# Seven-product units: two passes with the same weights as one product of 512 columns

## The chip, the core and the metric

The kernel runs on one core of one Trainium2 chip. The metric is the device time of one execution in microseconds; before the change it is 1432.15 us, the median of three runs from 1432.05 to 1433.4. Five engines work side by side: PE (TensorE, matmuls), DVE (VectorE), ACT (ScalarE), POOL (GpSimd) and SP, which here issues loads. Each goes through its own list of instructions in order and waits on semaphores for the others.

## What is computed

Two decoder layers over 512 tokens of 1024 channels, in float32. Layer 0 begins with a recurrent and pooling mixer, layer 1 with a convolution module; each layer then has cross-attention into 256 memory tokens and a gated MLP, which is the part that the change is about. Cut to it:

```
D_MODEL, SEQ, D_FF = 1024, 512, 3 * 1024

def rms_norm(x, g):
    y = x * rsqrt(mean(x * x, -1) + EPS)
    return y * g

def conv_ffn(x, norm, w_up, dw_w, dw_b, w_down):
    h = rms_norm(x, norm) @ w_up                       # 1024 -> 6144
    g = causal_dwconv(h[..., :D_FF], dw_w, dw_b)       # width 3
    u = h[..., D_FF:]
    return (gelu(g) * u) @ w_down

x = x + conv_ffn(x, ...)
```

## The kernel before

Activations are held transposed: 128 channels on the partitions, 512 tokens along the free dimension, eight such chunks `X[c]`. A float32 product is made of three products of a shorter format. Each operand is split into a high part (ACT copies it into that format, helper `high`) and a low part (DVE subtracts the high part from the operand, helper `low`); `mm3` then adds high x high, high x low and low x high into one PSUM bank, each by a matmul of its own.

The up projection of the MLP goes over 24 chunks of 128 gate channels, each with its 128 value channels. The first two chunks of a layer (`PLAIN`) are projected plainly in `opening`, by `start`. The other 22 are *units*, `unit(c)` for c from 2 to 23; `first` is 2 and `second` is 3. A unit treats gate and value weights as a 2 x 2 matrix of blocks (a11, a12, a22 and sums of blocks named s1 to s4) against a 2 x 2 matrix of token halves and channel halves of the normalised activations (B11, B21, B22 and sums T1 to T4, made once a layer by `Seven.sums`), and does with seven block products of 256 columns what takes eight otherwise. `Seven.product` adds the four chunks of one block product by four `mm3`.

The seven products of a unit go into three accumulators in PSUM: `G` (a11 with B11, then a12 with B21), `F` (starts as a copy of `G` after a11, made by ACT; then s2 with T2, s3 with T3, a22 with T4) and `H` (s1 with T1, then s4 with B22). Between the products, `F` and `H` are read out: after s2 into `u[:, :M]`, after s3 into `u[:, M:]`, and the halves of the gate `g` and the value `f` are put together from them. On PE the order in a unit is: H s1, F s2, G a12, F s3, the down projection of an earlier group of chunks (24 matmuls of 512 columns into two `aux` banks), the next unit's a11, H s4, F a22. `gating(c, ...)` is a generator that finishes chunk c in pieces during unit c + 1: it scales by the token norm `norm.r`, applies the causal convolution of width 3 (one ACT instruction, two on DVE), GeLU on ACT, the product with the value, and the split into `ys[c]`, which the down projection reads.

The weights of coming units are loaded by SP; ACT and DVE split each block; POOL starts DMAs that add one block onto another in place (in `Blocks.low`), which makes the sums s1 to s4. ACT also carries `X` into the down projection's bank and out again.

Inside `unit` and `opening` the order on PE, ACT, DVE and POOL is the order of the code (`tc.manual_schedule(engines=ORDERED)`): no engine takes an instruction ahead of one that is written earlier. `attention` uses the same class (there called `six`) for three of its four heads, and its products stay at 256 columns; its two plain `query` products and the plain products in `start` read the normalised activations `norm.x` and are touched by the new layout.

Of the kernel before, what the change touches and what calls it, by code (L numbers as in the profile page):

```python
# [15 lines left out]
P = 128  # L16
# [45 lines left out]
def trunk(ctx: ExitStack, tc: tile.TileContext, I: dict, out: list):  # L62
# [148 lines left out]

    class Norm:
# [257 lines left out]
    def attention(layer, norm, mem, nxt, six, up):  # L470
# [259 lines left out]
    class Seven:  # L730
# [11 lines left out]
        def fourth(self, k):  # L742
            split(self.t4[:, k * M : (k + 1) * M], *[x[:, M:] for x in self.norm.x[k]])

        def sums(self, k, between=None):
# [17 lines left out]
            for (hi, _), t in zip(self.t, (t1, t2, t3, t4)):  # L763
                A.activation(hi[:, at], t, AF.Copy)
            yield
            for (hi, lo), t in zip(self.t, (t1, t2, t3, t4)):
                V.tensor_tensor(lo[:, at], t, hi[:, at].bitcast(F32), op=ALU.subtract)

        def product(self, ps, w, j, first=True):
            for c in range(4):  # L770
                if j - self.T1 == len(self.t):
                    x = blk(self.norm.x[c], M, M)
                elif j >= self.T1:
                    x = blk(self.t[j - self.T1], c * M, M)
# [60 lines left out]
    def ffn(layer, norm, nxt, seven, pairs):  # L835
# [66 lines left out]

        def gating(c, g, f, u, F, H):
            add(g[:, right_half], H, u[:, :M])
            V.tensor_tensor(g[:, right_half], g[:, right_half], norm.r[:, right_half], op=ALU.mult)
# [3 lines left out]
            times_r(f, F, left_half)  # L909
# [14 lines left out]
        def ahead(c):  # L924

            G, F = main_ps()[:, :M], main_ps()[:, :M]
            m(c, G, "a11", seven.B11)
            A.activation(F, G, AF.Copy)
            return G, F

        def unit(c):
# [4 lines left out]
            H = main_ps()[:, :M]  # L936
# [9 lines left out]
            A.activation(u[:, :M], F, AF.Copy)  # L946
# [27 lines left out]
            V.tensor_tensor(f[:, right_half], f[:, right_half], norm.r[:, right_half], op=ALU.mult)  # L974
# [11 lines left out]
            if c >= GC - 1 and c + 1 in downs:  # L986
# [7 lines left out]
            low(c + 1, "s2")  # L994
            if down:
# [12 lines left out]
        def opening():  # L1008
# [4 lines left out]
            def start(i, ks=range(C)):  # L1013
                if ks[0] == 0:
                    ps[i] = main_ps()
                for k in ks:
                    mm3(ps[i], blk(w[i], k * P), norm.x[k], k == 0, k == C - 1)
# [21 lines left out]
            start(0, range(C - 1))  # L1039
            start(1, range(2))  # L1040
            start(0, (C - 1,))
# [9 lines left out]
            start(1, range(2, C))  # L1051
# [13 lines left out]
            start(2)  # L1065
# [11 lines left out]
            start(3)  # L1077
# [820 lines left out]
```

## Time and profile before

| | |
|---|---|
| median of three runs | 1432.15 us |
| the profiled execution | 1431.55 us |
| its span, first to last instruction | 1429.8 us |
| mean granted TensorE clock | 0.999 |
| PE busy | 1417.3 us (99%) |
| DVE busy | 1074.0 us (75%) |
| ACT busy | 900.6 us (63%) |
| POOL busy | 316.9 us (22%) |

A row of the profile gives an engine, a line, an operation, what it writes and reads with the shapes, how often, the busy time and the mean of one. `[2.58 <-PE mm L188]` means that the engine stood idle for 2.58 us before the instruction and that what ended it was PE's matmul of line 188 into `mm`. A row in order of time begins with its start in microseconds. The two MLPs' units take from about 380 to 710 us and from about 1070 to 1396 us of the span.

### The profile page before, as it was taken

How to read it: one execution, taken by the hardware profiler on the slowest of the kernel's cores; microseconds unless marked ns; L12 is line 12 of the kernel's file. 1: busy time of each engine (PE TensorE's matmuls, PEld its weight loads, DVE VectorE, ACT ScalarE, POOL GpSimd, SP SyncE). 2: the span in 40 equal slices, each digit the busy share in tenths (PEclk: the TensorE clock that was granted, in tenths of full speed). 3: DMA queues.
4: the chain of work that ended last, by engine and by line, in shares of the span. 5: the costliest groups of instructions: out<-in, count | busy, mean ns of one | idle time of the engine just before them, and what ended most of it. 6: DMA issues, size and time to landing. Idle time of an engine off the chain costs nothing.

```text
span 1429.8 us, 22834 instructions
## 1 busy us (share of the span) xinstructions
PE 1417.3 (99%) x8650; PEld 1261.6 (88%) x8650; DVE 1074.0 (75%) x1796; ACT 900.6 (63%) x1592; POOL 316.9 (22%) x333
## 2 busy tenths in 40 slices
PE   9999999999999999999999999999999999999998
PEld 7888888998999999999988777899889999999997
DVE  6987776778776676667798997978787676676665
ACT  7678754667555666666665547667665665666664
POOL 0011310210122222222008992010002222222111
PEclk9999999999999999999999999999999999999999
DMA  8522232544487777777432354345438777777741
GB/s 303 195 75 103 89 124 76 119 110 147 99 199 165 171 172 166 168 171 167 133 133 89 119 162 148 108 87 139 118 86 197 175 177 164 170 175 164 175 120 60
DMA packets 80031, 204.33 MB, mean 143 GB/s; under 512 B 9008, under 2 KB 9520, under 8 KB 79920
## 3 DMA queue, kind: packets, MB, share of 16 engines
q1 hardware_dynamic: 50832, 150.15, 32.8%
q0 software_dynamic: 28800, 52.44, 21.5%
q8 instruction: 68, 1.11, 0.3%
q14 instruction: 43, 0.35, 0.1%
q10 hardware_dynamic: 288, 0.27, 0.1%
HBM read 145.16 MB, written 2.10 MB: 103 GB/s over the span
## 4 chain that ended last, share of the span: by engine, by line
PE 89%; DVE 4%; POOL 2%; ACT 2%; issue 1%; DMA 1%; SPq 0%; POOLq 0%; DVEq 0%; ACTq 0%
PE mm L188 21%; PE mm L186 21%; PE mm L187 21%; PE aux L187 7%; PE aux L186 7%; PE aux L188 7%; PE mm L458 2%; DVE wlo L167 1%; DMA raw<-in_wv 1%; POOL actf L1498 1%; ACT whi L166 1%; PE aux L532 0%; POOL act L167 0%; POOL tmp L1319 0%; DMA raw<-in_wo 0%
## 5 line engine op out<-in xcount | busy, mean ns | idle before, releaser
L186 PE MATMUL mm<-act,whi 128*128 128x512 f32 (+2 forms) x1061 | 368.9, 349 | 0.7 <-ACT act L274 0.6
L187 PE MATMUL mm<-act,whi 128*128 128x512 f32 (+2 forms) x1061 | 369.1, 348 | 0.3 <-DVE act L181 0.2
L188 PE MATMUL mm<-act,wlo 128*128 128x512 f32 (+2 forms) x1061 | 369.0, 348 | 0.0
L186 PEld LDWEIGHTS mm<-act,whi 128*128 128x128 f32 x1061 | 200.5, 189 | 28.3 <-ACT act L274 1.3
L187 PEld LDWEIGHTS mm<-act,whi 128*128 128x128 f32 x1061 | 200.7, 189 | 27.4 <-DVE act L167 1.0
L188 PEld LDWEIGHTS mm<-act,wlo 128*128 128x128 f32 x1061 | 200.7, 189 | 25.1 <-DVE wlo L167 0.6
L822 DVE TENSOR_TENSOR bigr<-raw,bigr 128x512 fp32r<-128x512 f32 x176 | 120.8, 688 | 131.6 <-ACT bigr L815 127.9
L188 PE MATMUL mm<-bigr,bigr 128*128 128x256 f32 x704 | 199.4, 283 | 1.7 <-DVE bigr L822 1.7
L186 PE MATMUL mm<-bigr,bigr 128*128 128x256 f32 x704 | 199.2, 283 | 0.0
L187 PE MATMUL mm<-bigr,bigr 128*128 128x256 f32 x704 | 199.2, 283 | 0.0
L815 ACT ACTIVATE bigr<-raw 128x512 fp32r<-128x512 f32 x176 | 109.0, 621 | 79.1 <-DVE wlo L203 75.9
L828 POOL DMA_DIRECT2D raw<-wa x100 | 87.9, 899 | 309.0 <-DVE bigr L822 215.2
L186 PE MATMUL aux<-act,whi 128*128 128x512 f32 x399 | 155.7, 390 | 0.0
L187 PE MATMUL aux<-act,whi 128*128 128x512 f32 x399 | 155.7, 390 | 0.0
L188 PE MATMUL aux<-act,wlo 128*128 128x512 f32 x399 | 155.2, 389 | 0.0
L166 ACT ACTIVATE whi<-raw 128x1024 fp32r<-128x1024 f32 (+1 forms) x95 | 96.5, 1020 | 87.6 <-PE mm L187 45.2
L188 PEld LDWEIGHTS mm<-bigr,bigr 128*128 128x128 f32 x704 | 135.1, 192 | 2.1 <-DVE bigr L822 2.1
L186 PEld LDWEIGHTS mm<-bigr,bigr 128*128 128x128 f32 x704 | 135.2, 192 | 0.0
L187 PEld LDWEIGHTS mm<-bigr,bigr 128*128 128x128 f32 x704 | 135.2, 192 | 0.0
L825 POOL DMA_DIRECT2D raw<-raw x50 | 43.2, 864 | 366.5 <-DVE wlo L822 347.3
L167 DVE TENSOR_TENSOR wlo<-raw,whi 128x1024 fp32r<-128x1024 f32 (+1 forms) x75 | 90.3, 1210 | 19.5 <-ACT whi L166 19.0
L188 PEld LDWEIGHTS aux<-act,wlo 128*128 128x128 f32 x399 | 74.9, 188 | 15.8
(353 smaller groups left out, 3040.8 us busy)
## 6 DMA issues: line engine op xcount, KB each, us to landing
raw<-wa POOLq DMA_DIRECT2D x150, 256.0 KB, 3.4
wa<-in_wpair SPq DMA_DIRECT2D x88, 256.0 KB, 3.7
raw<-in_wpair SPq DMA_DIRECT2D x44, 512.0 KB, 3.8
big<-in_wdown SPq DMA_DIRECT2D x42, 512.0 KB, 4.4
raw<-raw POOLq DMA_DIRECT2D x50, 256.0 KB, 3.7
raw<-in_pw SPq DMA_DIRECT2D x24, 512.0 KB, 3.3
raw<-in_win SPq DMA_DIRECT2D x20, 512.0 KB, 3.3
raw<-in_wk SPq DMA_DIRECT2D x16, 512.0 KB, 3.3
```

Source lines behind the costliest of these rows:

```text
L166: A.activation(hi, src, AF.Copy)
L167: fetched[1] = (eng or V).tensor_tensor(lo, src, hi.bitcast(F32), op=ALU.subtract)
L186: PE.matmul(ps, wh, xh, start=first, stop=False, skip_group_check=onto)
L187: PE.matmul(ps, wh, xl, start=False, stop=False, skip_group_check=onto)
L188: return PE.matmul(ps, wl, xh, start=False, stop=last, skip_group_check=onto)
L458: PE.matmul(p, m[j], x, start=k == 0 and j == 0 and x is hi, stop=k == C - 1 and x is lo)
L815: A.activation(self.w[name][0], self.block(name), AF.Copy)
L822: V.tensor_tensor(lo, self.block(name), hi.bitcast(F32), op=ALU.subtract)
L825: G.dma_start(self.r, self.z, accum_op=ALU.add)
L828: G.dma_start(block, self.a22, accum_op=ALU.add)
L1498: G.tensor_tensor(z[:, s:], z[:, s:], f[:, s:], op=ALU.add)
```

## The change

A block of activations (its high part, 256 columns, and its low part, 256 columns) now lies side by side in one tile of 512 columns. In the units above `second` (4 to 23, in both layers) an accumulator is a whole bank of 512 columns. The high part of a weight block is multiplied with both parts in one matmul of 512 columns: the left half of the bank collects high x high, the right half high x low. The low part of the weights is multiplied with the high part alone, 256 columns, into the left half. An accumulator's value is therefore the sum of its halves, and wherever it is read, `gather` first copies the right half out with ACT and then adds the left half with DVE. The units 2 and 3 and the attention keep three matmuls of 256 columns. Since `norm.x` is laid out by token halves, the plain products in `query` and `start` go half by half, with twice as many matmuls of half the width. A norm's copy and subtraction are made in two halves each. Two first units of the new form have one extra matmul onto the `F` bank ahead of its copy. The order of the down weights' split moves in unit `second`.

```
     class Norm:
         def feed(self, c):
             g = col(self.gain[0], self.gain[1] + c)
-            hi, lo = act_r(), act_r()
-            A.activation(hi, X[c], AF.Copy, scale=g)
-            self.last = V.scalar_tensor_tensor(lo, X[c], g, hi.bitcast(F32), op0=ALU.mult, op1=ALU.subtract)
-            self.x[c] = (hi, lo)
+            self.x[c] = act_r(), act_r()
+            halves = [(parts(x), X[c][:, i * M : (i + 1) * M]) for i, x in enumerate(self.x[c])]
+            for (hi, _), x in halves:
+                A.activation(hi, x, AF.Copy, scale=g)
+            for (hi, lo), x in halves:
+                self.last = V.scalar_tensor_tensor(lo, x, g, hi.bitcast(F32), op0=ALU.mult, op1=ALU.subtract)
...
         def query(n, w):
             ps = mm_ps()
-            for i, k in enumerate(PAIRED):
-                mm3(ps, blk(w, k * P), norm.x[k], i == 0, i == C - 1)
+            for half in range(2):
+                for i, k in enumerate(PAIRED):
+                    mm3(parts(ps)[half], blk(w, k * P), parts(norm.x[k][half]), i == 0, i == C - 1)
...
         def product(self, ps, w, j, first=True):
             for c in range(4):
...
+                (wh, wl), x = blk(w, c * P), self.block(j, c)
+                if ps.shape[-1] == T:
+                    steps = [(ps, wh, x), (ps[:, :M], wl, x[:, :M])]
+                    for i, (to, part, by) in enumerate(steps if c < 3 else steps[::-1]):
+                        PE.matmul(
+                            to, part, by, start=first and c == 0 and i == 0, stop=c == 3 and i == 1, skip_group_check=True
+                        )
                 else:
-                    x = blk(self.norm.x[c if j == self.B11 else c + 4], M if j == self.B22 else 0, M)
-                mm3(ps, blk(w, c * P), x, first and c == 0, c == 3, not first)
+                    mm3(ps, (wh, wl), parts(x), first and c == 0, c == 3, not first)
...
+        def gather(out, ps):
+            A.activation(out, ps[:, M:], AF.Copy)
+            add(out, ps[:, :M], out)
+
         def gating(c, g, f, u, F, H):
-            add(g[:, right_half], H, u[:, :M])
-            V.tensor_tensor(g[:, right_half], g[:, right_half], norm.r[:, right_half], op=ALU.mult)
+            if c > second:
+                gather(g[:, right_half], H)
+                add(g[:, right_half], g[:, right_half], u[:, :M])
+                V.tensor_tensor(g, g, norm.r, op=ALU.mult)
...
             yield
-            times_r(f, F, left_half)
+            if c > second:
+                gather(f[:, left_half], F)
+                V.tensor_tensor(f, f, norm.r, op=ALU.mult)
...
         def ahead(c):
-            G, F = main_ps()[:, :M], main_ps()[:, :M]
+            G = bank(c)
+            F = bank(c) if c > second else parts(main_ps())[1]
             m(c, G, "a11", seven.B11)
+            if c in (second + 1, second + 2):
+                w = pairs[c].w["a11"]
+                PE.matmul(F, w[0][:, :P], seven.block(seven.B11, 0), start=True, stop=True)
             A.activation(F, G, AF.Copy)
...
             m(c, F, "s2", seven.T2, False)
-            A.activation(u[:, :M], F, AF.Copy)
+            if c > second:
+                A.activation(f[:, right_half], H[:, M:], AF.Copy)
+                gather(u[:, :M], F)
...
             if c > second:
-                times_r(g, G, left_half)
+                gather(g[:, left_half], G)
             m(c, F, "s3", seven.T3, False)
-            A.activation(u[:, M:], F, AF.Copy)
-            add(f[:, right_half], H, u[:, M:])
+            if c > second:
+                gather(u[:, M:], F)
+                add(f[:, right_half], f[:, right_half], u[:, M:])
+                add(f[:, right_half], H[:, :M], f[:, right_half])
...
-            V.tensor_tensor(f[:, right_half], f[:, right_half], norm.r[:, right_half], op=ALU.mult)
+            if c <= second:
+                V.tensor_tensor(f[:, right_half], f[:, right_half], norm.r[:, right_half], op=ALU.mult)
```

Where this moves instructions, in three places. First DVE, from the end of one unit to the first read of `F` in the next, in layer 0; before, with `mm_5972` and `mm_5929` that unit's `H` and `F`, `tmp_6002` its `g`, `tmp_6001` its `f`, `tmp_6146` the convolution:

```order
L822 TENSOR_TENSOR bigr_6099<-raw_5732,bigr_6099 128x512
L171 TENSOR_TENSOR tmp_6002<-mm_5972,tmp_6000 128x256
L905 TENSOR_TENSOR tmp_6002<-tmp_6002,r_3611 128x256
L887 TENSOR_TENSOR tmp_6001<-mm_5929,r_3611 128x256
L898 SCALAR_TENSOR_TENSOR tmp_6146<-tmp_6002,par,tmp_6146 128x511
L898 SCALAR_TENSOR_TENSOR tmp_6146<-tmp_6002,par,tmp_6146 128x510
L822 TENSOR_TENSOR bigr_6185<-raw_5908,bigr_6185 128x512
```

and with the change, where `mm_5924` and `mm_5891` are the unit's `H` and `F`, `tmp_5948` its `g`, `tmp_5947` its `f`, `tmp_6078` the convolution, and `mm_6047` and `tmp_6102` the next unit's `F` and `u`:

```order
L840 TENSOR_TENSOR bigr_6041<-raw_5714,bigr_6041 128x512
L171 TENSOR_TENSOR tmp_5948<-mm_5924,tmp_5948 128x256
L171 TENSOR_TENSOR tmp_5948<-tmp_5948,tmp_5946 128x256
L930 TENSOR_TENSOR tmp_5948<-tmp_5948,r_3706 128x512
L171 TENSOR_TENSOR tmp_5947<-mm_5891,tmp_5947 128x256
L939 TENSOR_TENSOR tmp_5947<-tmp_5947,r_3706 128x512
L916 SCALAR_TENSOR_TENSOR tmp_6078<-tmp_5948,par,tmp_6078 128x511
L916 SCALAR_TENSOR_TENSOR tmp_6078<-tmp_5948,par,tmp_6078 128x510
L171 TENSOR_TENSOR tmp_6102<-mm_6047,tmp_6102 128x256
L840 TENSOR_TENSOR bigr_6113<-raw_5870,bigr_6113 128x512
```

The next unit's `F` is now read by DVE too, and that add stands behind the two convolution instructions of the unit before; between the reading of `H` and the convolution stand two more instructions, and the scalings are 512 columns wide.

The same place on ACT; before, from the high part of s2 (which waits for DVE's low part of the down weights in both versions) to the GeLU:

```order
L815 ACTIVATE bigr_5923<-raw_5556 128x512
L860 ACTIVATE x<-aux_5828 128x512
L928 ACTIVATE mm_5929<-mm_5928 128x256
L860 ACTIVATE x<-aux_5830 128x512
L895 ACTIVATE tmp_5970<-tmp_5826,par 128x512
L946 ACTIVATE tmp_6000<-mm_5929 128x256
L855 ACTIVATE aux_6004<-x 128x512
L855 ACTIVATE aux_6006<-x 128x512
L900 ACTIVATE tmp_5970<-tmp_5970 128x512
```

and with the change:

```order
L833 ACTIVATE bigr_6041<-raw_5714 128x512
L878 ACTIVATE x<-aux_5952 128x512
L964 ACTIVATE mm_6047<-mm_6046 128x512
L878 ACTIVATE x<-aux_5954 128x512
L923 ACTIVATE tmp_5948<-mm_5924 128x256
L913 ACTIVATE tmp_6078<-tmp_5948,par 128x512
L923 ACTIVATE tmp_5947<-mm_5891 128x256
L986 ACTIVATE tmp_6103<-mm_6080 128x256
L923 ACTIVATE tmp_6102<-mm_6047 128x256
L873 ACTIVATE aux_6108<-x 128x512
L873 ACTIVATE aux_6110<-x 128x512
L918 ACTIVATE tmp_6078<-tmp_6078 128x512
```

Ahead of the convolution's first tap (L895, now L913) stands the copy of `H`'s right half, behind it the copies of `F`'s, `H`'s and the next `F`'s, and the copy that starts `F` is 512 columns wide.

Third, half a product on PE (`G` with a12), before:

```order
L186 MATMUL mm_5752<-act_3297,whi_5525 128x256
L187 MATMUL mm_5752<-act_3298,whi_5525 128x256
L188 MATMUL mm_5752<-act_3297,wlo_5526 128x256
L186 MATMUL mm_5752<-act_3398,whi_5525 128x256
L187 MATMUL mm_5752<-act_3399,whi_5525 128x256
L188 MATMUL mm_5752<-act_3398,wlo_5526 128x256
```

and a whole one with the change, up to the first matmul of `F` with s3:

```order
L791 MATMUL mm_5578<-act_3330,whi_5371 128x512
L791 MATMUL mm_5578<-act_3330,wlo_5372 128x256
L791 MATMUL mm_5578<-act_3407,whi_5371 128x512
L791 MATMUL mm_5578<-act_3407,wlo_5372 128x256
L791 MATMUL mm_5578<-act_3512,whi_5371 128x512
L791 MATMUL mm_5578<-act_3512,wlo_5372 128x256
L791 MATMUL mm_5578<-act_3618,wlo_5372 128x256
L791 MATMUL mm_5578<-act_3618,whi_5371 128x512
L791 MATMUL mm_5579<-bigr_3304,bigr_5489 128x512
```

Twelve matmuls of 256 columns have become four of 512 and four of 256. Over the program PE has 1664 matmuls of 256 columns fewer and 836 of 512 more; DVE has 192 instructions more and ACT 192.

More of the change, by code (lines that the diff above doesn't have):

```diff
@@ L209, in blk, with parts @@
         return hi[:, i : i + n], lo[:, i : i + n]
+    def parts(x):
+        return x[:, :M], x[:, M:]
     class Norm:
@@ L742, in fourth @@
         def fourth(self, k):
-            split(self.t4[:, k * M : (k + 1) * M], *[x[:, M:] for x in self.norm.x[k]])
+            split(self.t4[:, k * M : (k + 1) * M], *parts(self.norm.x[k][1]))
         def sums(self, k, between=None):
@@ L985, in unit @@
                 pairs[c + 2].load_second()
-            if c >= GC - 1 and c + 1 in downs:
+            if c > second and c + 1 in downs:
                 downs[c + 1].w.high()
@@ L994, in unit @@
             low(c + 1, "s2")
+            if c == second:
+                downs[c + 1].w.high()
+                downs[c + 1].w.low()
             if down:
@@ L1011, in opening, with start @@
             ps, y = {}, {}
-            def start(i, ks=range(C)):
-                if ks[0] == 0:
+            def start(i, half, ks=range(C)):
+                if half == 0 and ks[0] == 0:
                     ps[i] = main_ps()
                 for k in ks:
-                    mm3(ps[i], blk(w[i], k * P), norm.x[k], k == 0, k == C - 1)
+                    mm3(parts(ps[i])[half], blk(w[i], k * P), parts(norm.x[k][half]), k == 0, k == C - 1)
             def fetch(i):
@@ L1038, in opening @@
             ss = split(norm.ss)
-            start(0, range(C - 1))
-            start(1, range(2))
-            start(0, (C - 1,))
+            start(0, 0, range(C - 1))
+            start(1, 0, range(C - 1))
+            start(0, 0, (C - 1,))
             fetch(2)
@@ L1050, in opening @@
             V.reciprocal(norm.r, root)
-            start(1, range(2, C))
+            start(1, 0, (C - 1,))
+            start(0, 1)
+            start(1, 1)
             pairs[second].load()
@@ L1063, in opening @@
             next(g, None)
-            start(2)
+            start(2, 0)
+            start(2, 1)
             both(second, "a11")
```

36 lines of the change are left out of this document (26 added, 10 removed).

## The prediction

> **What bounds the kernel now.** I read the page's shares first, then what PE waits for, then one unit's rows, engine by engine.
>
> ```profile
> span 1429.8 us, 22834 instructions
> PE 1417.3 (99%) x8650; PEld 1261.6 (88%) x8650; DVE 1074.0 (75%) x1796; ACT 900.6 (63%) x1592; POOL 316.9 (22%) x333
> PE mm L188 <- DVE bigr L822: 1.7, 2, 0.8
> 435.44:699.61 264.17, 264.17 (x1838) 247.87 (x1837) 178.00 (x305) 163.22 (x306) 57.01 (x66) 1.00 0.71 166
> ```
>
> PE is busy nearly all the time, and its longest wait in the whole run sums to 1.7 us. The last row is a stretch of 17 units: PE 264.17 of 264.17 us at a granted clock of 1.00, DVE 178.00, ACT 163.22. So a unit lasts as long as its matmuls take:
>
> ```profile
> 561.11 0.40 PE L186 MATMUL aux<-act,whi 128*128 128x512 f32 x1
> 566.58 0.28 PE L186 MATMUL mm<-act,whi 128*128 128x256 f32 x1
> 573.77 0.28 PE L186 MATMUL mm<-act,whi 128*128 128x256 f32 x1
> 575.21 0.28 PE L186 MATMUL mm<-bigr,bigr 128*128 128x256 f32 x1
> 576.65 0.40 PE L186 MATMUL aux<-act,whi 128*128 128x512 f32 x1
> 419.89 0.62 ACT L900 ACTIVATE tmp<-tmp 128x512 f32<-128x512 f32 x1
> 699.61 0.62 ACT L900 ACTIVATE tmp<-tmp 128x512 f32<-128x512 f32 x1
> ```
>
> The starts are to be read, not the modelled 0.28 and 0.40. From 573.77 to 575.21 stands one product (`G` with a12) of 12 matmuls of 256 columns: 0.120 us each. From 561.11 to 566.58 stand the 24 of 512 columns of the down projection: 5.47 us, 0.228 each (0.227 away from their first two). A matmul is thus nearly in proportion to its columns: two of 256 take 0.240, one of 512 takes 0.227. The two GeLU rows lie 18 units apart: 279.72 / 18 = 15.54 us a unit, which is 7 x 1.44 + 5.46.
>
> What PE hides is how closely DVE and ACT follow. One unit of each:
>
> ```profile
> 576.46 0.69 DVE L822 TENSOR_TENSOR bigr<-raw,bigr 128x512 fp32r<-128x512 f32 x1 [3.50 <-ACT bigr L815]
> 577.07 0.68 DVE L914 SCALAR_TENSOR_TENSOR tmp<-tmp,tmp 128x512 f32<-128x512 f32 x1
> 578.46 0.69 DVE L919 TENSOR_TENSOR act<-tmp,act 128x512 fp32r<-128x512 f32 x1 [0.70 <-ACT act L917]
> 579.07 0.68 DVE L822 TENSOR_TENSOR bigr<-raw,bigr 128x512 fp32r<-128x512 f32 x1
> 579.67 0.42 DVE L887 TENSOR_TENSOR tmp<-mm,r 128x256 f32<-128x256 f32 x1
> 580.00 0.41 DVE L171 TENSOR_TENSOR tmp<-mm,tmp 128x256 f32<-128x256 f32 x1
> ...
> 582.47 1.22 DVE L203 TENSOR_TENSOR wlo<-big,whi 128x1024 fp32r<-128x1024 f32 x1
> ...
> 585.19 0.42 DVE L171 TENSOR_TENSOR tmp<-mm,tmp 128x256 f32<-128x256 f32 x1
> 585.65 0.42 DVE L905 TENSOR_TENSOR tmp<-tmp,r 128x256 f32<-128x256 f32 x1
> 586.63 0.42 DVE L887 TENSOR_TENSOR tmp<-mm,r 128x256 f32<-128x256 f32 x1 [0.56 <-PE mm L188]
> 586.98 1.53 DVE L898 SCALAR_TENSOR_TENSOR tmp<-tmp,par,tmp 128x511 f32<-128x511 f32 x2
> ```
>
> ```profile
> 573.97 0.38 ACT L946 ACTIVATE tmp<-mm 128x256 f32<-128x256 f32 x1 [2.58 <-PE mm L188]
> 574.25 1.11 ACT L855 ACTIVATE aux<-x 128x512 f32<-128x512 f32 x2
> 575.29 0.62 ACT L900 ACTIVATE tmp<-tmp 128x512 f32<-128x512 f32 x1
> 575.82 0.62 ACT L815 ACTIVATE bigr<-raw 128x512 fp32r<-128x512 f32 x1
> 577.79 0.63 ACT L917 ACTIVATE act<-tmp 128x512 fp32r<-128x512 f32 x1 [0.84 <-DVE tmp L914]
> 583.72 0.63 ACT L815 ACTIVATE bigr<-raw 128x512 fp32r<-128x512 f32 x1 [2.00 <-DVE wlo L203]
> 584.26 0.58 ACT L860 ACTIVATE x<-aux 128x512 f32<-128x512 f32 x1
> 584.74 0.38 ACT L928 ACTIVATE mm<-mm 128x256 f32<-128x256 f32 x1
> 585.04 0.59 ACT L860 ACTIVATE x<-aux 128x512 f32<-128x512 f32 x1
> 586.11 0.82 ACT L895 ACTIVATE tmp<-tmp,par 128x512 f32<-128x512 f32 x1 [0.48 <-DVE tmp L905]
> 590.84 0.62 ACT L900 ACTIVATE tmp<-tmp 128x512 f32<-128x512 f32 x1
> ```
>
> The two engines hand work to each other in a loop that closes once a unit: convolution (586.98), GeLU, high and low part of s3, gated product, `ys`, s4, the run of low parts up to the down weights (L203, 582.47), which the high part of s2 on ACT waits for (583.72), then `g` (585.19), its scaling, the convolution's first tap on ACT (586.11), convolution. The only slack: the convolution pair ends at 586.98 + 1.53 = 588.51, its GeLU could start at 588.55 and starts at 590.84, since ACT stands before it, waiting for PE (L946, 2.58). So the loop needs 15.54 - 2.29 = **13.25 us** of its own. Busy shares of 75% and 63% do not show that.
>
> **The change, part by part.** *PE gives up* 28 matmuls in each of the 40 units above `second`: 28 x (0.240 - 0.227) = 0.36 us a unit, so PE's need falls to 7 x 4 x 0.347 + 5.46 = 15.18. Over the kernel that is 1120 x 0.013 = 14.6 us. *PE takes on* the halved products: 24 more matmuls in each of 4 queries and 8 opening products, 288 x 0.013 = 3.7 us, and 4 priming matmuls of 0.227, 0.9 us. PE alone: -10 us.
>
> The Trainium skill, "TensorE: Matmul & The Clock Gate", section "Back-to-back issue gap", gives a warm gap of columns/2.4 GHz plus about 2.5 ns. By that an instruction saved is worth 2.5 ns and not the 13 of these rows, and PE alone would come out at -1 us (828 fewer instructions, 2.1, less the priming). The rows decide; the rule speaks against the change all the same.
>
> *DVE and ACT take on* the gathers. `F` is read three times a unit, and where ACT alone read it into `u`, ACT now copies the right half and DVE adds the left. That matters at one place: the next product onto `F` (T3 with s3) overwrites what the read needs, so PE must now wait for a DVE instruction that stands in DVE's queue behind the previous unit's whole convolution (first order fence above). Before, it waited for ACT's L946 alone, which starts at 573.97 and is read out 0.86 us before the product's 575.21.
>
> The low parts on DVE also set off POOL's accumulating DMAs, which make the sums that s2 and s4 are taken from:
>
> ```profile
> raw<-wa POOLq DMA_DIRECT2D x150, 256.0 KB, 3.4
> ```
>
> From s3's low part to s2's high part there are 583.72 - 576.46 = 7.26 us now and 2.00 + 4.59 + 1.25 = 7.84 in the walk below, against 3.4 to land: these DMAs stay covered, at no cost. Unit `second` does the down weights' split behind s1 and s2 instead of ahead of them, the same instructions on ACT and DVE, with their product a unit away: 0.
>
> The new loop, walked along the queues of the changed order, in durations of the rows above:
> - convolution pair 1.53, handover 0.04, GeLU 0.53 (575.29 to 575.82), s3 high to low 0.64 (575.82 to 576.46): 2.74.
> - s3 low to `ys` low, 576.46 to 578.46: 2.00.
> - `ys` low and s4 low 0.61 + 0.60; gather into `g` 0.33 (579.67 to 580.00); gather into `u` and the add that needs it 0.46 each (585.19 to 585.65); add of `H` 0.33; low parts a22, a11, a12 3 x 0.60: 4.59. Before, 578.46 to 582.47 was 4.01.
> - down weights' low to s2's high on ACT, 582.47 to 583.72: 1.25.
> - on ACT s2 0.54, copy out 0.48, the copy into `F`, now 512 wide, 0.53, copy out 0.51: 2.06.
> - the gather of `H` 0.42 (ACT, 0.38 + 0.04), two adds 0.46 each, a 512-wide scaling 0.69 + 0.04, first tap 0.82 - 0.08 until ACT is free, gather of `F` 0.42 + 0.46, scaling 0.60, to the convolution: 4.29. Before, these last two points and the tap were 583.72 to 586.98, 3.26.
>
> Sum **16.93 us** against PE's 15.18: the loop decides, and PE stands about 1.7 us a unit ahead of T3 with s3. The gather that PE waits for falls into the DVE time between convolution and s3 low, so it adds nothing to the loop. In the 36 units between the quoted GeLU rows and their like in layer 1: 36 x (16.93 - 15.54) = **+50 us**. The units at the ends of each layer (4 and 23) get part of it, 0 to 1.4 each: +3. The halved products: +3.7. The longer gating after the last unit, two more steps of 0.4 and a 512-wide scaling, before the last down products: 0 to 2.5 a layer, I take +2. The halved norm copies add up to 32 x 0.2 = 6 us on DVE outside the units, where PE does not wait now: 0 (2 if the cover is short). The priming disappears in the stalls. Sum +59 on the profiled execution's 1431.55, which lies 0.6 under the median: **1491 us**.
>
> The Trainium skill, "PSUM — Partial Sum Buffer", section "Engine vs sequencer instructions", calls the ACT and DVE queues strictly first in, first out. The waits in the rows above fit that; it is what carries the stall to PE.
>
> **Rivals.** *PE alone counts*, as it does now: the gathers fit into DVE's 25% and ACT's 37% idle time. For it: PE's 99%, no wait. Against it: 2.29 us of slack, and the loop grows by 3.68. It decides from a loop under 15.18 on, that is if 1.75 of the 3.68 us of new steps ran beside others in the same queues. 1431.55 - 10 = **1422**. The skill's "Perfetto Trace Analysis", section "Identifying Performance Opportunities", would have the most-contended engine improved first; that is this rival.
>
> *The short loop*: s2's high part gets a buffer that is free earlier, so ACT's queue runs ahead of DVE there. Then the loop closes over PE: three products 3 x 1.39 and the down projection 5.46 from T3 to the end of `H`; 0.20 until ACT sees it (573.77 to 573.97), 0.42 + 0.46 + 0.46 + 0.73 + 0.74 + 0.42 + 0.46 + 0.60, the pair up to its next instruction 1.45, gather 0.46: 16.03. 36 x 0.49 + 9 = +27: **1458**. Against it: the changed program has the same wait there on DVE (second place in the order).
>
> *A longer loop*: every added read of PSUM also delays the others, the loop reaches 17.4, 36 x 1.86 + 9: **1508**.
>
> *The products don't merge in time*: 512 columns cost two times 256, PE gains nothing; the loop still decides, so the time is the forecast's.
>
> **Numbers.** Forecast (1480 to 1502) 0.66, short loop 0.14, PE alone 0.11, longer loop 0.07, no change 0.02. A measurement here can tell about 0.2%. Faster 0.11, same 0.02, slower 0.87. The range takes in the short loop and most of the longer one: 1457 to 1506.
>
> **What would show it.** Right: matmuls of 512 columns at 0.227 and 256 at 0.120 within a product; units 16.9 apart; PE idle about 1.7 us a unit, ended by a DVE add into `u`; DVE's idle ahead of s3 low down from 3.50 to about 1 us; ACT's wait on PE ahead of the gather near 0. Wrong: units 15.2 apart, with PE still at 99%; or PE's wait ending on ACT; or a stall at the s1 and s2 products, on weights.

## The result and the profile after

| | before | after |
|---|---|---|
| median | 1432.56 us (4 runs, 1432.05 to 1433.4) | 1499.51 us (4 runs, 1497.31 to 1500.29) |
| ratio | | 1.0466, 95% interval 1.0453 to 1.0479 |
| span of the profiled execution | 1429.8 us | 1497.5 us |
| mean granted TensorE clock | 0.999 | 0.996 |

The change makes the kernel 67 us slower. The forecast was 1491 us (1457 to 1506).

First the shares of the span and the chain that ended last, on the page of the changed kernel:

```profile
span 1497.5 us, 21630 instructions
PE 1428.6 (95%) x7822; PEld 1219.3 (81%) x7822; DVE 1167.9 (78%) x1988; ACT 963.4 (64%) x1784; POOL 317.3 (21%) x333
PE 40%; DVE 31%; ACT 16%; issue 7%; DMA 3%; POOL 2%; SPq 0%; DVEq 0%; ACTq 0%; POOLq 0%
```

PE has 828 instructions fewer and DVE and ACT have 192 more each. The chain is no longer PE alone: DVE and ACT hold 47% of it, although the page shows them busy for 78% and 64% only. What PE waits for (sum in us, times, longest):

```profile
PE mm L791 <- DVE tmp L171: 50.8, 40, 1.3
PE mm L791 <- ACT mm L964: 2.1, 2, 1.1
```

Forty waits, one in each unit of the new form, ended by a DVE add. Seventeen units lie between the next two rows (the GeLU of two units, ACT in order of time), and the window below covers the same stretch (us, then busy time of PE, PEld, DVE, ACT and POOL, then PE's granted clock):

```profile
426.16 0.63 ACT L918 ACTIVATE tmp<-tmp 128x512 f32<-128x512 f32 x1 [0.82 <-DVE tmp L916]
713.68 0.63 ACT L918 ACTIVATE tmp<-tmp 128x512 f32<-128x512 f32 x1 [0.99 <-DVE tmp L916]
```

```profile
426.00:714.00 288.00, 265.25 (x1361) 222.38 (x1361) 217.06 (x376) 187.78 (x375) 58.81 (x68) 1.00 0.65 156
```

287.52 / 17 = **16.91 us a unit**, where it was 15.54 and the prediction had 16.93. No engine is saturated: PE 265 of 288, DVE 217, ACT 188. One unit on DVE, and the places of it on ACT that DVE waits for or that wait for DVE:

```profile
576.75 1.53 DVE L916 SCALAR_TENSOR_TENSOR tmp<-tmp,par,tmp 128x511 f32<-128x511 f32 x2
578.20 0.42 DVE L171 TENSOR_TENSOR tmp<-mm,tmp 128x256 f32<-128x256 f32 x1
579.56 0.69 DVE L840 TENSOR_TENSOR bigr<-raw,bigr 128x512 fp32r<-128x512 f32 x1 [0.94 <-ACT bigr L833]
...
581.55 0.69 DVE L951 TENSOR_TENSOR act<-tmp,act 128x512 fp32r<-128x512 f32 x1 [0.70 <-ACT act L949]
...
586.15 1.22 DVE L203 TENSOR_TENSOR wlo<-big,whi 128x1024 fp32r<-128x1024 f32 x1
...
589.83 0.42 DVE L171 TENSOR_TENSOR tmp<-mm,tmp 128x256 f32<-128x256 f32 x1 [1.06 <-ACT tmp L923]
...
593.66 1.53 DVE L916 SCALAR_TENSOR_TENSOR tmp<-tmp,par,tmp 128x511 f32<-128x511 f32 x2
595.10 0.42 DVE L171 TENSOR_TENSOR tmp<-mm,tmp 128x256 f32<-128x256 f32 x1
```

```profile
578.38 0.63 ACT L918 ACTIVATE tmp<-tmp 128x512 f32<-128x512 f32 x1 [1.00 <-DVE tmp L916]
578.91 0.61 ACT L833 ACTIVATE bigr<-raw 128x512 fp32r<-128x512 f32 x1
...
587.40 0.63 ACT L833 ACTIVATE bigr<-raw 128x512 fp32r<-128x512 f32 x1 [2.31 <-DVE wlo L203]
587.94 0.58 ACT L878 ACTIVATE x<-aux 128x512 f32<-128x512 f32 x1
588.42 0.59 ACT L964 ACTIVATE mm<-mm 128x512 f32<-128x512 f32 x1
588.94 0.59 ACT L878 ACTIVATE x<-aux 128x512 f32<-128x512 f32 x1
589.42 0.38 ACT L923 ACTIVATE tmp<-mm 128x256 f32<-128x256 f32 x1
591.47 0.82 ACT L913 ACTIVATE tmp<-tmp,par 128x512 f32<-128x512 f32 x1 [1.68 <-DVE tmp L930]
```

The loop of the prediction can be read off term by term, each from one start to the next:

| stretch of the loop | forecast | read |
|---|---|---|
| convolution to s3's low part, 576.75 to 579.56 | 2.74 | 2.81 |
| s3's low part to `ys` low, to 581.55 | 2.00 | 1.99 |
| `ys` low to the down weights' low part, to 586.15 | 4.59 | 4.60 |
| to s2's high part on ACT, 587.40 | 1.25 | 1.25 |
| to the gather of `H` on ACT, 589.42 | 2.06 | 2.02 |
| to the next convolution, 593.66 | 4.29 | 4.24 |
| sum | 16.93 | 16.91 |

And PE at the place where it stalls:

```profile
576.72 0.40 PE L791 MATMUL mm<-act,wlo 128*128 128x256 f32 x2
576.96 0.39 PE L791 MATMUL mm<-act,whi 128*128 128x512 f32 x1
578.67 1.66 PE L791 MATMUL mm<-bigr,bigr 128*128 128x512 f32 x8 [1.32 <-DVE tmp L171]
```

T3 with s3 (578.67) starts when DVE's add of the two halves of `F` (578.20, 0.42 long) has landed. That add stands in DVE's queue directly behind the convolution (576.75).

### The profile page after: what moved, and what is told of

Its sections match the earlier page's. It is cut to its first block, busy times and chain, and to the rows that moved or that the text cites. A ratio compares the mean times of both kernels' runs of the same rounds, so it can differ in the third digit from the quotient of the medians.

```text
span 1497.5 us, 21630 instructions
## 1 busy us (share of the span) xinstructions
PE 1428.6 (95%) x7822; PEld 1219.3 (81%) x7822; DVE 1167.9 (78%) x1988; ACT 963.4 (64%) x1784; POOL 317.3 (21%) x333
## 4 chain that ended last, share of the span: by engine, by line
PE 40%; DVE 31%; ACT 16%; issue 7%; DMA 3%; POOL 2%; SPq 0%; DVEq 0%; ACTq 0%; POOLq 0%
PE mm L186 11%; PE mm L187 11%; PE mm L188 10%; DVE tmp L171 7%; DVE bigr L840 5%; DVE tmp L916 4%; DVE wlo L203 3%; ACT bigr L833 3%; ACT x L878 2%; DVE wlo L840 2%; ACT tmp L913 2%; DVE tmp L939 2%; DVE tmp L930 2%; ACT act L949 2%; PE aux L188 2%
## 5 line engine op out<-in xcount | busy, mean ns | idle before, releaser
L186 PE MATMUL mm<-act,whi 128*128 128x512 f32 (+2 forms) x837 | 295.4, 355 | 2.2 <-ACT act L279 1.5
L187 PE MATMUL mm<-act,whi 128*128 128x512 f32 (+2 forms) x837 | 296.3, 354 | 0.1
L188 PE MATMUL mm<-act,wlo 128*128 128x512 f32 (+2 forms) x837 | 295.8, 353 | 0.0
L791 PE MATMUL mm<-bigr,bigr 128*128 128x512 f32 (+1 forms) x1280 | 244.1, 343 | 52.9 <-DVE tmp L171 50.8
L791 PEld LDWEIGHTS mm<-bigr,bigr 128*128 128x128 f32 x1280 | 198.6, 188 | 94.0 <-DVE tmp L171 63.5
L171 DVE TENSOR_TENSOR tmp<-mm,tmp 128x256 f32<-128x256 f32 x290 | 118.0, 420 | 86.5 <-ACT tmp L923 83.3
L186 PEld LDWEIGHTS mm<-act,whi 128*128 128x128 f32 x837 | 158.2, 189 | 24.9 <-ACT act L279 2.2
L187 PEld LDWEIGHTS mm<-act,whi 128*128 128x128 f32 x837 | 158.5, 189 | 22.7 <-DVE act L167 1.0
L188 PEld LDWEIGHTS mm<-act,wlo 128*128 128x128 f32 x837 | 158.5, 189 | 21.3 <-DVE wlo L167 0.6
L791 PE MATMUL mm<-act,whi 128*128 128x512 f32 x320 | 119.4, 397 | 0.0
L913 ACT ACTIVATE tmp<-tmp,par 128x512 f32<-128x512 f32 x48 | 39.2, 816 | 78.7 <-DVE tmp L930 68.2
L187 PEld LDWEIGHTS aux<-act,whi 128*128 128x128 f32 x399 | 74.9, 188 | 16.0
```

The lines of the kernel that those rows point to most:

```text
L171: V.tensor_tensor(out, a, b, op=ALU.add)
L186: PE.matmul(ps, wh, xh, start=first, stop=False, skip_group_check=onto)
L187: PE.matmul(ps, wh, xl, start=False, stop=False, skip_group_check=onto)
L188: return PE.matmul(ps, wl, xh, start=False, stop=last, skip_group_check=onto)
L791: PE.matmul(to, part, by, start=first and c == 0 and i == 0, stop=c == 3 and i == 1, skip_group_check=True)
L913: A.activation(y, g, AF.Identity, scale=dw(2), bias=col("f_dw_b", layer * CF + c))
```

## The experiments

**Without the gathers, and without the wide products.** In the first, all that remains of a gather is a read of the left half, and the scalings go back to 256 columns:

```
         def gather(out, ps):
-            A.activation(out, ps[:, M:], AF.Copy)
-            add(out, ps[:, :M], out)
+            A.activation(out, ps[:, :M], AF.Copy)
...
-                gather(g[:, left_half], G)
+                times_r(g, G[:, :M], left_half)
```

> The changed kernel, but wherever an accumulator of a wide unit is read, only its left half is read, with the instructions of the kernel before (no gather, ACT alone copies F out). PE's list is unchanged. Left out of the result: high x low in units 4 to 23. Theory (the gathers make the loop over DVE and ACT too long, the merged products are cheap): the loop falls back to about 13.3 to 13.5 us, PE's 15.18 decide, units 15.2 apart, 1420 to 1427 us. Rival (wide products themselves cost more than 0.347 a pair, or full banks make PE wait): 1436 us or more, units over 15.5 apart. Rival (gathers only part of it): 1440 to 1480.

Measured: 1433.64 us, ratio 1.001 (1.0001 to 1.0019). The gathers, with the wider scalings that came with them, are the whole loss: without them PE's waits in the units are gone. But PE alone does not win 10 us either. Two GeLU rows eighteen units apart, and the starts of a run of three products on PE:

```profile
422.36 0.62 ACT L918 ACTIVATE tmp<-tmp 128x512 f32<-128x512 f32 x1
698.35 0.62 ACT L918 ACTIVATE tmp<-tmp 128x512 f32<-128x512 f32 x1
```

```profile
569.92 4.40 PE L791 MATMUL mm<-bigr,bigr 128*128 128x512 f32 x24
574.16 0.40 PE L791 MATMUL mm<-act,whi 128*128 128x512 f32 x1
```

275.99 / 18 = 15.33 us a unit, not 15.18. The 12 pairs of 512 and 256 columns take 4.24 us, 0.353 a pair, not 0.347. So a merged pair saves 7 ns and not 13, and a unit 0.21 us and not 0.36.

In the second, the units are narrow again and the rest of the change stays (each test of `c > second` in the units goes the same way):

```
         def bank(c):
-            return main_ps() if c > second else main_ps()[:, :M]
+            return main_ps() if False else main_ps()[:, :M]
```

> The changed kernel with units 4 to 23 made of three matmuls of 256 columns as before; what is left of the change is the layout by token halves, the halved plain products, the norm copies in two halves and the moved split of the down weights in unit 3. Theory: 288 more matmuls of 0.013 us = +3.7 us and 0 to 2 for the norm copies, 1435.5 to 1438 us, units 15.54 apart. Rival (the opening of a layer, where 2 to 3 us more than forecast appeared, is late because of the new layout): 1440 to 1444 us.

Measured: 1436.0 us, ratio 1.0033 (1.002 to 1.0045), units 15.54 apart. +3.9 us by the medians, as the term of the halved products had it (3.7).

**The slack of the kernel before.** Nothing of the change is in these two; DVE repeats a subtraction that stands in the loop, once more in the first and, with range(3), three times more in the second:

```
                 downs[c + 1].w.high()
                 downs[c + 1].w.low()
+                for _ in range(1):
+                    downs[c + 1].w.low()
```

> The kernel before, with the subtraction of the down weights' low part on DVE made twice over in units 3 to 23: 1.2 us more for DVE at a place inside the loop. Theory (a loop of 13.25 us under PE's 15.54, slack 2.29): 13.25 + 1.2 = 14.45 is still below, 0 to +3 us, 1432 to 1435. Rival (each added DVE or ACT step shows in the time): 42 x 1.2 = +50, 1482.

> The kernel before, with the same subtraction made four times over: 3.6 us more for DVE a unit, about as much as the loop grew by in the change (3.68), with nothing else of the change. Theory (loop): 13.25 + 3.6 to 3.8 = 16.85 to 17.05 against 15.54, +1.3 to +1.5 in 42 units and something at the ends, 1485 to 1505 us, PE waiting on DVE though DVE is busy for only about 14 of 17 us. Rival (busy time decides): DVE needs 10.5 + 3.6 = 14.1 us a unit, less than PE's 15.54: no change, 1432 to 1436.

Measured: 1440.46 us (ratio 1.0056, 1.0043 to 1.007) with one, 1506.24 us (1.0521, 1.0507 to 1.0535) with three. With one, the units do not move at all; the next rows are 17 units apart, 264.18 / 17 = 15.54:

```profile
439.51 0.62 ACT L900 ACTIVATE tmp<-tmp 128x512 f32<-128x512 f32 x1
703.69 0.62 ACT L900 ACTIVATE tmp<-tmp 128x512 f32<-128x512 f32 x1
```

So 1.2 us of added DVE work a unit cost nothing where the slack covers it, and the slack shrinks by about as much:

```profile
592.15 1.54 DVE L898 SCALAR_TENSOR_TENSOR tmp<-tmp,par,tmp 128x511 f32<-128x511 f32 x2 [0.55 <-ACT tmp L895]
594.91 0.62 ACT L900 ACTIVATE tmp<-tmp 128x512 f32<-128x512 f32 x1
```

The convolution pair ends at 593.69, so the GeLU could start at 593.73 and starts at 594.91: 1.18 of the 2.29 us are left.

The 8 us that came all the same, against the 0 to 3 expected, lie outside the units that are in step. The profiled execution (2.0 us above the median) is 10.9 us longer than that of the kernel before. Of these, 1.3 us are there ahead of the first repeat, at layer 0's first GeLU (371.34 against 370.00), and so are not of its making; 4.1 at unit 4's GeLU (423.98 against 419.89), 4.1 still at unit 23's (717.35 against 713.29), 8.0 at the first GeLU of layer 1 (1065.88 against 1057.91) and 10.7 at its unit 4 (1117.97 against 1107.29). In each of the three places where the distance grows, PE first waits and then works at a lower granted clock: 0.57 from 404 to 408 us, 0.66 from 748 to 753 and from 1096 to 1101. By the starts of the same matmuls in both kernels, PE falls back by 1.4, 1.5 and 1.4 us in these slow stretches, 4.3 of the 10.9. The loop theory said nothing of those places.

With three, PE waits for DVE in 40 units, in a kernel with narrow products and no gather:

```profile
PE mm L188 <- DVE bigr L822: 56.7, 40, 4.6
```

```profile
427.00:700.00 273.00, 251.50 (x1720) 232.93 (x1720) 224.01 (x336) 153.72 (x288) 55.61 (x64) 1.00 0.65 154
```

Units are 17.09 apart (sixteen of them in the window, which begins and ends at a GeLU), where 16.85 to 17.05 was expected, and the time is a little above 1505. PE is busy for 251.5 of 273 us, DVE for 224: busy time explains neither, a loop does. It is not quite the loop of the prediction, though:

```profile
581.95 0.69 DVE L822 TENSOR_TENSOR bigr<-raw,bigr 128x512 fp32r<-128x512 f32 x1 [1.67 <-ACT bigr L815]
592.87 1.28 DVE L822 TENSOR_TENSOR bigr<-raw,bigr 128x512 fp32r<-128x512 f32 x2
599.03 0.69 DVE L822 TENSOR_TENSOR bigr<-raw,bigr 128x512 fp32r<-128x512 f32 x1 [1.66 <-ACT bigr L815]
```

```profile
593.61 0.39 PE L188 MATMUL mm<-bigr,bigr 128*128 128x256 f32 x1 [1.29 <-DVE bigr L822]
596.54 0.38 ACT L946 ACTIVATE tmp<-mm 128x256 f32<-128x256 f32 x1 [0.74 <-PE mm L188]
```

The repeats stand right ahead of s1's and s2's low parts, which PE needs. From s3's low part (581.95) to the first of these two (592.87) there are 10.92 us, to the matmul that waits for it 0.74, over two products to ACT's copy of `F` 2.93, and over the GeLU to the next s3 low part 2.49: 17.08. The convolution pair, which is in the prediction's loop, ends at 597.38 and the GeLU starts at 597.86, so that way round has 0.44 us to spare here.

**Shortening the loop of the changed kernel.** No instruction is added or taken away in the first three. s3's high part goes ahead of the GeLU on ACT:

```
+            high(c + 1, "s3")
             next(left, None)
-            both(c + 1, "s3")
+            low(c + 1, "s3")
```

> The changed kernel; ACT makes the high part of s3 ahead of the GeLU instead of behind it, so that DVE's low part of s3 runs beside the GeLU. No instruction is added or left out. Theory (a loop over DVE and ACT of 16.93 us in which GeLU, s3 high and s3 low stand one behind the other): about 1.1 us of it (s3 high 0.53 and s3 low 0.60) leave the loop, 15.8 us; the loop over PE of 16.03 (the rival called short loop) is then the longer one: units 16.0 apart, 36 x 0.9 = 33 us less, 1460 to 1468. Rival (PE's wait on the gather of F is the cost by itself, 40 x 1.3 = 51 us): order elsewhere changes nothing, 1496 to 1501.

ACT's copies of the down projection's banks into X (L878) go behind the gather of `H` and the scaling, just ahead of the first tap:

```
-            if down:
-                down.home(0, d[0], seeded)
...
-            left = gating(c, g, f, u, F, H)
+            def homes():
+                if down:
+                    for i in range(2):
+                        down.home(i, d[i], seeded)
+
+            left = gating(c, g, f, u, F, H, homes)
```

> The changed kernel; ACT's two copies of the down projection's banks into X stand behind the gather of H instead of ahead of it. No instruction is added or left out. Theory (they lie in the loop with 0.48 and 0.51 us, and behind the gather ACT waits for DVE anyway): the loop falls by 1.0 to 15.9, the loop over PE of 16.03 takes over: 1458 to 1466 us. Rival (PE's wait is the cost by itself): 1496 to 1501.

Both at once:

> The changed kernel with both moves (s3's high part ahead of the GeLU, copy outs behind the gather of H). Theory (two loops): the loop over DVE and ACT is down to 14.8, but the one over PE stays: T3 with s3 waits for DVE's gather, which stands behind the convolution, which needs H of the unit before. Units still 15.9 to 16.1 apart, 1456 to 1465 us, no better than one move alone by more than 5 us. Rival (one loop only): 14.8 lies under PE's 15.33, the wait goes, 1433 to 1440 us.

| | median | ratio (95%) | us a unit |
|---|---|---|---|
| s3's high part early | 1472.17 | 1.0279 (1.0262 to 1.0295) | 16.16 |
| copy outs later | 1470.15 | 1.0266 (1.0249 to 1.0284) | 16.16 |
| both | 1470.81 | 1.0269 (1.0254 to 1.0284) | 16.16 |

Moving one instruction in ACT's list, or two, gives back 27 to 29 us, so PE's wait on the gather is not a price by itself. The two moves together are worth no more than either: there is a second loop, of 16.16 us, which neither shortens. The times came 4 to 6 us above the expected ranges, since 16.0 had been taken for 16.16. The second loop shows in the run with both moves; ACT's gather of `H` now waits for PE (the prediction's walk had ACT late there, with no wait):

```profile
571.00 1.68 PE L791 MATMUL mm<-bigr,bigr 128*128 128x512 f32 x8 [0.56 <-DVE tmp L171]
```

```profile
580.99 0.39 ACT L923 ACTIVATE tmp<-mm 128x256 f32<-128x256 f32 x1 [0.83 <-PE mm L791]
```

From T3 with s3 (571.00) PE runs to the end of `H`, which ACT sees at 580.99, 9.99 us on; the gather of `H`, the scaling, the tap, the gather of `F`, the convolution and the gather into `u` follow, and the next T3 with s3 starts 16.16 after the last.

This loop goes through PE's wait on DVE. Let ACT free `F` instead:

```
-                gather(u[:, :M], F)
+                whole = tmp_f()
+                A.activation(whole, F, AF.Copy)
+                add(u[:, :M], whole[:, :M], whole[:, M:])
```

> The changed kernel; after s2 ACT copies the whole bank of F (512 columns) into SBUF and DVE adds the two halves there, so PE's T3 with s3 waits for ACT alone. The buffer that s2's high part gets is then no longer the one of the down weights (it is one that PE frees). Prediction's theory (the loop does not go over PE): with the wait on the down weights' low gone the loop still has DVE's whole list of low parts in it: about 16 us a unit, 1454 to 1464. Rival (PE's wait alone was the cost): 15.33 a unit, 1433 to 1440. Rival (the wait only moves): 16.9, 1495 to 1500.

Measured: 1463.12 us, ratio 1.0218 (1.0203 to 1.0233), units 15.99 apart, as the first theory of the expectation had it (about 16). It is neither the 15.33 of "PE's wait alone" nor the unchanged 16.91 of "it only moves". The edit also changes which buffer s2's high part gets, and ACT waits there for PE and not for the down weights' low part any more:

```profile
ACT bigr L833 <- PE mm L791: 51.3, 36, 1.9
```

So it undoes two links at once, and its gain cannot be split between them in this run. A buffer of its own for s2's high part, which would undo the one link alone, was not tried.

**All three moves.**

> The changed kernel with three moves at once: s3's high part ahead of the GeLU, the copy outs behind the gather of H, and ACT copying the whole bank of F after s2 (DVE adds the halves in SBUF). All gathers are still made. Theory (two loops, 16.93 over DVE and ACT and 16.16 over PE): both fall below what PE needs, which is 15.33 a unit as measured without gathers; units 15.3 to 15.4 apart, PE without a wait in them; 36 x 0.8 less than the 1470 of either move, and up to 5 us of the ends: 1435 to 1443 us, so still not faster than before. Rival (DVE and ACT are simply too full with the gathers, DVE 226 of 280 us): units stay at 15.9 or more, 1460 or more.

Measured: 1438.46 us, ratio 1.0041 (1.0027 to 1.0055). Seventeen units of it:

```profile
424.00:685.00 261.00, 261.00 (x1364) 222.77 (x1363) 216.74 (x375) 190.45 (x375) 58.68 (x68) 1.00 0.72 172
```

PE is busy throughout, units are 15.33 apart as without gathers, and DVE does the same work as in the changed kernel at 83% instead of 75%. All gathers fit once the loops are short enough. In this kernel the edit that frees `F` leaves the buffer of s2's high part as it was; ACT waits for the down weights' low part, with the same sum as in the run with both moves (87.6 us):

```profile
ACT bigr L833 <- DVE wlo L203: 87.6, 38, 2.3
```

So the step from both moves (16.16) to all three (15.33) is the freeing of `F` alone. 61 of the 67 us are back by order and by one read alone.

In the next, the four matmuls of 512 columns of a product come first, then the four of 256:

```
-            for c in range(4):
...
-                    for i, (to, part, by) in enumerate(steps if c < 3 else steps[::-1]):
+                for i in (0, 1):
+                    for c in range(4):
+                        by = self.block(j, c)
+                        to, by = (ps[:, :M], by[:, :M]) if i else (ps, by)
```

> As the run with the three moves, and in each wide product the four matmuls of 512 columns first, then the four of 256, instead of by turns. Same matmuls. Theory A (the 0.353 of a pair, measured against 0.227 + 0.120 = 0.347, comes from the turns between 512 and 256): units 15.15 to 15.2 apart, 6 us less, 1429 to 1437 us. Theory B (it is a cost of a 512-column or 256-column matmul here, whatever its neighbour): units 15.3 to 15.4 apart, the same time within 2 us.

Measured: 1436.13 us, ratio 1.0027 (1.0016 to 1.0038), units 15.27 apart. Between the two theories: the turns account for 0.07 of the 0.15 us a unit that were missing. The rest lies with the wide matmuls: over its units one of 512 columns followed by its like takes 0.233 us, against 0.228 in the down projection, and one of 256 takes 0.118. Why is open.

Last, the same with unit 23 of each layer narrow:

```
-            return main_ps() if c > second else main_ps()[:, :M]
+            return main_ps() if second < c < CF - 1 else main_ps()[:, :M]
```

> As the run with the three moves and grouped products, but the last unit of each layer (23) is made of three matmuls of 256 columns again, so that its gating has no gathers. In the run before it the GeLU of unit 22 is 1.4 us ahead of the kernel before the change and that of unit 23 is 2.15 us behind it. Theory (the longer gating after the last unit stands before the last down products with nothing beside it, the prediction's tail term, mis-sized at +2 for both layers): PE pays 2 x 0.28 for the unit and 2 to 3 us come back in each layer, 1430.5 to 1434. Rival (the ends are late because products were moved between the layers' ends and the norm, which the gathers have nothing to do with): 1435 to 1437.5, no change.

Measured: 1434.1 us, ratio 1.0018 (1.0009 to 1.0027). In layer 0 the GeLU of unit 23 follows that of unit 22 after 14.24 us (699.92 to 714.16), where it took 17.24 (698.20 to 715.44): 3 us back in that stretch. Of the time, 2 us: it lies just above the 1430.5 to 1434 of the theory, and the intervals of the two ratios overlap, so the gain on the whole is likely but not settled. No version that was run beats the kernel before.

## Why the prediction was right, and which terms were off

**The loop**: right, in its sum (16.91 against 16.93) and in each of its six stretches to within 0.07 us. DVE's idle ahead of s3's low part went from 3.50 to 0.94, ACT's wait on PE ahead of the gather into `u` from 2.58 to none, and PE loses 16.91 - 15.33 = 1.58 us a unit at the wait that the add into `u` ends (the rows show 1.3 of it, counted from the modelled end of a matmul). The 36 units cost 24.1 us in each layer (unit 4 to unit 22: 303.83 against 279.72 us), 48 in all; the forecast was 50.

**The slack of 2.29 us before**: borne out by the run with one repeat, where 1.2 us added leave the units at 15.54 and 1.18 us of slack. Three repeats bring the units to 17.09, but over another loop, so that run shows that a loop decides and not the size of this slack.

**s2's high part waits for the down weights' low part**: right, 2.31 us in the rows above. The rival of the *short loop*, "over PE at 16.03", was no invention: it is there at 16.16 and decides as soon as the longer one is cut. The difference is that of its three products: two take 1.41 us instead of 1.39, and T3 with s3, just behind PE's wait, takes 1.52 (to 588.67 from 587.15, one unit after the row at 571.00), 0.17 together; the rest of the loop is 0.04 shorter than its sum.

**"Two of 256 take 0.240, one of 512 takes 0.227", 13 ns saved**: the step that failed. The two numbers came from rows in which all neighbours were of one kind, and the 512 columns from another product. Within a product the pair takes 0.353 and not 0.347, so a unit saves 0.21 us and not 0.36, 8 us over the 40 units and not 14.6, and the rival *PE alone* was worth 1433.6 us and not 1422: no gain, even if the gathers cost nothing. The price of the pair is 6 of these 11.6 us; the turns between the two widths make up 0.07 of its 0.15 us a unit, and the rest is not explained. In the profiled execution of that run, 0.4 us shorter than the one of the kernel before, the 36 units save 7.4 us and the rest of the program loses 7.0, where the halved products and the priming had been put at 4.6; the median lies 2.5 us above that execution, and why is open. The forecast did not rest on this term, since the loop decides. The Trainium skill, "TensorE: Matmul & The Clock Gate", section "Back-to-back issue gap", had led to -1 us for PE alone, nearer to the +1.5 measured than the -10 from the rows. Its 2.5 ns a matmul is not what these rows show, though, and that section of the Trainium skill calls the formula the gap of an isolated matmul, without the weight load that each matmul of a stream has. So it came nearer by luck. A unit with 28 matmuls fewer is 0.21 us shorter, 7 ns each.

**+3.7 for the halved products**: +3.9 measured by the medians. (Its profiled execution, in the table below, lies 1.4 above its median, that of the kernel before 0.6 below its own.)

**+3 for units 4 and 23, +2 for the gating after the last unit**: too small. The GeLU starts of four kernels, from ACT's rows in order of time, each with its distance from the kernel before:

| place | before | after | narrow units | three moves, grouped |
|---|---|---|---|---|
| layer 0, unit 4 | 419.89 | 426.16 (+6.3) | 422.43 (+2.5) | 423.78 (+3.9) |
| layer 0, unit 22 | 699.61 | 729.99 (+30.4) | 702.15 (+2.5) | 698.20 (-1.4) |
| layer 0, unit 23 | 713.29 | 748.29 (+35.0) | 715.76 (+2.5) | 715.44 (+2.2) |
| layer 1, first chunk | 1057.91 | 1095.91 (+38.0) | 1060.19 (+2.3) | 1063.73 (+5.8) |
| layer 1, unit 4 | 1107.29 | 1150.28 (+43.0) | 1113.14 (+5.9) | 1116.65 (+9.4) |
| layer 1, unit 22 | 1387.01 | 1454.09 (+67.1) | 1392.86 (+5.9) | 1391.08 (+4.1) |

Beyond what the narrow units show there too, the changed kernel loses 3.7 us up to unit 4 in layer 0, 7.9 from unit 22 to layer 1's first chunk, 1.4 up to unit 4 in layer 1 and nothing to speak of after its last unit: 13 us, where these two terms had 5. More than half of it is the end of layer 0: 4.7 us up to unit 23's GeLU (3 us came back there with that unit narrow, in the last experiment) and 3.2 in the stretch between the layers, below. What the openings lose was not tried by itself. With the 48 of the units and the 5.9 that the narrow units lose in their own profiled execution, these 13 make up the 67 us, where the forecast had 50, 3.7 and 5.

**The rivals**: *a longer loop* (17.4) and *no merging* did not come; matmuls of 512 and 256 columns stand in the rows as 0.23 and 0.12.

## What to carry to other kernels

Where PE is at 99%, look for the loop that the other engines close once an iteration and measure its slack before giving them work, since their busy shares do not show it: 1.2 us more on DVE left the units where they were, and 3.6 us more cost as much as this whole change, with DVE idle for a fifth of the time. Once a loop decides, look at the order of the two engines' lists before the number of their instructions (one ACT copy, the high part of s3, moved: 27 us), and expect that behind the longest loop a second may lie close by. A price per matmul is to be read from rows of the product and with the neighbours that it will have.

## What the runs showed of the hardware

**The granted clock falls after some stalls of PE, and not after one a unit.** Between the layers a product of the memory's keys, which filled PE's gap at the norm before (its matmuls went on to 740.16 us, past the norm's sums at 735.72), now runs ahead of it (to 769.80, with the sums at 770.95). PE's waits there and slices of 10 us, one of layer 0's opening and two of this place (busy time of PE, then of the others, the granted clock third from the end):

```profile
770.95 1.05 PE L319 MATMUL stat<-onesf,tmp 128*128 128x1 f32 x8 [0.86 <-DVE tmp L253]
773.50 1.59 PE L355 MATMUL aux<-act,unit 128*128 128x512 f32 x2 [1.50 <-DVE act L332]
776.59 0.80 PE L186 MATMUL mm<-act,whi 128*128 128x512 f32 x1 [1.50 <-ACT act L279]
```

```profile
400.00:410.00 10.00, 7.69 (x50) 6.55 (x49) 7.32 (x13) 4.22 (x8) 2.59 (x3) 1.00 0.86 208
...
770.00:780.00 10.00, 6.14 (x19) 4.04 (x19) 7.53 (x15) 4.31 (x8) 0.00 (x0) 0.67 0.08 31
780.00:790.00 10.00, 10.00 (x50) 8.51 (x49) 5.60 (x9) 3.67 (x6) 0.00 (x0) 0.98 0.00 0
```

Three waits of 3.86 us together within 6.5 us, and the mean clock of the slice is 0.67. In slices of 1 us the clock is 1.00 up to 773 us, 0.74 in the next, 0.50 from 774 to 780 and 0.84 in the one after: it fell as the second wait ended, and the third lies in the slow stretch already. In the kernel before with one repeated subtraction, a single wait of 2.08 us in layer 0's opening goes with 0.83:

```profile
402.69 0.39 PE L188 MATMUL mm<-bigr,bigr 128*128 128x256 f32 x1 [2.08 <-DVE bigr L822]
```

```profile
400.00:410.00 10.00, 7.92 (x53) 7.71 (x52) 7.09 (x11) 4.29 (x9) 2.60 (x3) 0.83 0.77 164
```

In the units of the changed kernel, with a wait of 1.3 us every 16.91, it stays at 1.00; so it does in that kernel's slice from 400 to 410 us, where PE is idle for 2.31 us in all, in waits of 1.06 and 1.25. The Trainium skill, "TensorE: Matmul & The Clock Gate", section "What's actually happening", has the clock halved after an idle window of about 3.4 us; here 2.08 us of waiting were enough in one place. The cost can be read between the layers: the next layer's first nine matmuls, six of 512 columns and three of 256, take 3.67 us (776.59 to 780.26), where they took 2.34 before (741.04 to 743.38). These 1.3 us are nearly all of the 1.4 by which the changed kernel falls back from the norm's scaling on DVE (739.58 before, 775.12 after) to the next layer's first gate on ACT (753.53 and 790.43).

**A matmul's start-to-start time differs by some ns with its place.** In this kernel's format 256 columns take 0.120 us among their like and 512 take 0.227 in the down projection; by turns a pair takes 0.353 (0.235 and 0.117 in the run with the three moves), and with four of a kind in a row 28 pairs are 0.07 us shorter. So the neighbours account for part of the difference; why 0.08 us a unit still remain is open.
